# Sample attention: the scores of four sequences issued together, in the four column tiles of the array

## The chip, the cores and the metric

The kernel runs on one core of a Trainium2 chip. The metric is the device time of one launch in microseconds (us). The profiled execution has a time of its own, and its span runs from its first to its last instruction.

## The reference, cut to what matters

One inference step of a two-layer decoder for two request groups with shared weights: a prompt of 512 new tokens, and eight sequences (the sample) with 512 past tokens and four new ones each. Layer A has sparse attention (eight query heads in two key heads, `g` = 0 and 1) beside a gated linear recurrence, layer C is a second recurrence; then a norm. The change is in layer A's attention of the sample. For each sequence `b` and each of two kinds, keys and values come from a paged cache (kind 0, the selected blocks, which are all of them here) or from the sliding window (kind 1):

```python
s = jnp.einsum('qgrd,qgnkd->qgrnk', qg, ks).reshape(qb, HKV, GRP, n_top * L_SEL) * scale
p_s = masked_softmax(s, kpos <= tpos[:, None, None, None])
o_s = jnp.einsum('qgrm,qgmd->qgrd', p_s, vs.reshape(qb, HKV, n_top * L_SEL, DH))
...
s = jnp.einsum('qgrd,kgd->qgrk', qg, wk[:, 0]) * scale
p_w = masked_softmax(s, wmask[:, None, None, :])
o_w = jnp.einsum('qgrk,kgd->qgrd', p_w, wk[:, 1])
o = gx[..., 0:1] * o_c + gx[..., 1:2] * o_s + gx[..., 2:3] * o_w
```

A sequence has 8 heads x 4 tokens = 32 query rows, 16 for each key head; past keys and values have 512 rows of 2 x 128 numbers.

## The kernel before, in words

Everything is float32; the big projections split both operands into two float32r parts and add three products. A weight block is 2048 x 128, its result 128 x 544 (512 prompt tokens and 32 of the sample) in the PSUM tile `gm`. For each of the 16 slices of the contraction six matmuls of 272 columns are issued (`gemm_block`, a *product set* below), and behind each set stands `self.pump()`.

`pump` is a planner. It runs while the program is built and decides the order in which instructions enter the queues. All other work is written as Python generators in lanes; a generator yields the modelled time at which its next step may go (`at`: when the tiles that it reads are modelled as ready, 200 ns later; with `banks` when so many of the four PSUM banks `s` are free). The planner's clock `clk` advances by the modelled cost of each TensorE instruction; after every product set it runs each lane whose time has come. A matmul of at most 32 stationary columns with a `tile_position` is charged 26 + 0.42 n ns (`mm`), a transpose 109. `until` and `force` run the lanes with no products between when the stream can't go on. On the chip nothing of this clock is left: each engine runs its queue in the order written and waits on semaphores for what it reads.

`decode()` is one lane, started when the prompt's attention is done. It treats four items, (group of four sequences, kind) = (0, 0), (1, 0), (0, 1), (1, 1). In an item:

- The keys of a sequence are two page tiles of 128 x 2 x 256 (rows x pages x both key heads), loaded by SP. `fetch()` keeps at most PAGES = 9 tiles in flight or in use, and asks in the order of `feed`: the item's eight key tiles, its eight value tiles, then the next item. A tile counts until `del pages[...]`. A tile of kind 0 is two DMAs (a page each, its address read from the page table), one of kind 1 a single DMA.
- For each sequence `b` and head group `g` four transposes bring the keys to a bank as 128 x 512, a copy (`cp`: ScalarE or VectorE, whichever the planner sees free first) takes them to a tile `kct`, and `scores` multiplies: stationary the queries of the sequence, 128 x 32 (`qd`, zero where a row is of the other head group), moving `kct`, out 32 partitions x 512 of the bank `S`, in column tile `b % 4`. The two head groups add up in the same rows. The score of a step is issued after the copy of the next step (`pend`), so at most two `kct` live.
- Then softmax over `S` (`dm`, `dnm`, `pd`), transposes of `pd`, a copy `ptd`, and the value products, four sequences side by side in the four column tiles, `pg` = 0, 1 with the first half of the value tiles, 2, 3 with the second.

Tiles of type `r` share 17 granules (RGRAN): pages, `kct`, `qd`, `orow` and others, and four split key tiles of the prompt's attention, which `self.khl` holds. When the last item is done, `orow` is transposed, added into `odec`, and the flag `attention` is set; the heads are then gated and split into `oh` and `ol` (`parts`). The stream of blocks meanwhile goes through layer A's last gate projections and on to the output projection `out_blocks`, whose first block takes the recurrence's eight slices first and the eight heads last (`order_a`), and waits for their splits (`ahead_a`).

Of the kernel before, what the change touches and what calls it, by code (L numbers as in the profile page):

```python
# [94 lines left out]
class Kern:  # L95
# [1285 lines left out]
    def decode(self):  # L1381
        nc, ident, a = self.nc, self.ident, self.a
        yield from self.wait("ratt", "gates", "kv10", "kv11", "kvc00", "kvc01", "kvc10", "kvc11")
        yield from self.wait(*[f"pu{h}" for h in range(DECODE_AFTER + 1)])
        yield self.at(self.qd)
        self.odec = self.g("odec", [P, 256])
        orow = self.r("orow", [P, 2, P])
# [2 lines left out]
        for gr, kind in items:  # L1390
            bs = range(4 * gr, 4 * gr + 4)
            feed += [(kind, 0, b, hf) for b in bs for hf in range(2)] + [(kind, 1, b, hf) for hf in range(2) for b in bs]
        pages = {}

        def fetch():
            while feed and len(pages) < PAGES:
                kind, sl, b, hf = key = feed.pop(0)
                if kind == 0:
                    t = self.cache_tile(self.r, 2 + sl, b, hf)
                else:  # L1400
                    t = self.r("pw", [P, 2, 256])
                    src = a["cache_win"][0, b, hf * 256:(hf + 1) * 256, sl].rearrange("(k p) h d -> p k (h d)", p=P)
                    nc.sync.dma_start(t, src)
                pages[key] = t
# [18 lines left out]
        for gr in range(2):  # L1423
            yield self.at(banks=1)
            S = self.bank(reads=2)
            for bl in range(4):
                b = 4 * gr + bl
# [17 lines left out]
            ps = self.bank()  # L1445
# [15 lines left out]
        for gr, kind in items:  # L1461
            bs = list(range(4 * gr, 4 * gr + 4))
            yield self.at(banks=1)
            S = self.bank(reads=2)

            def scores(b, g, t):
                rows = slice(32 * (b % 4), 32 * (b % 4) + 32)
                self.mm(S[rows, :], self.qd[:, g, b, :], t[:, :TP], start=(g == 0), stop=(g == 1),
                        tile_position=(0, 32 * (b % 4)))

            pend = None
            for b in bs:
                ts = [pages[(kind, 0, b, hf)] for hf in range(2)]
                for g in range(2):
                    yield self.at(*ts, banks=1)
                    ps = self.bank()
                    for pg in range(4):
                        self.tr(ps[:, pg * P:(pg + 1) * P], ts[pg // 2][:, pg % 2, g * P:(g + 1) * P], ident)
                    if pend:
                        yield self.at(pend[2], ps)  # L1480
                    else:
                        yield self.at(ps)
                    t = self.r("kct")
                    self.cp(t[:, :TP], ps)
                    if pend:
                        scores(*pend)
                    pend = (b, g, t)
                for hf in range(2):
                    del pages[(kind, 0, b, hf)]
                fetch()  # L1490
            yield self.at(pend[2])
            scores(*pend)
            pend, t = None, None
            yield self.at(S)
            if kind == 1:
                nc.vector.tensor_tensor(S[:, 0:4], S[:, 0:4], self.winneg, op=ALU.add)
            m = self.sm("dm", [P, 2], bufs=2)
            pk = pn[:, gr, kind, :]
            nc.vector.tensor_reduce(m[:, 0:1], S, axis=AX.X, op=ALU.max)
            nc.vector.tensor_reduce(m[:, 1:2], pk, axis=AX.X, op=ALU.max)  # L1500
            nm = self.sm("dnm", [P, 1], bufs=2)
            nc.vector.tensor_reduce(nm, m, axis=AX.X, op=ALU.max, negate=True)
            yield self.at(nm)
            p = self.r("pd")
            s2 = self.sm("ds", [P, 2], bufs=2)
            nc.scalar.activation(p[:, :TP], S, AF.Exp, bias=nm, accum_out=s2[:, 0:1])
            nc.scalar.activation(p[:, TP:T], pk, AF.Exp, bias=nm, accum_out=s2[:, 1:2])
            yield self.at(p, s2)
            sm = self.sm("dsm", [P, 1], bufs=2)
            nc.vector.tensor_tensor(sm, s2[:, 0:1], s2[:, 1:2], op=ALU.add)  # L1510
            w = self.weigh(sm, self.gr[gr][:, 1 + kind:2 + kind])
            wm = self.sm("dwm", [P, 2], bufs=2)
            nc.vector.tensor_scalar(wm, self.gsel, w, None, op0=ALU.mult)
            yield self.at(banks=2)
            ps, ps2 = self.bank(), self.bank()
            for j in range(4):
                self.tr(ps[:, j * P:(j + 1) * P], p[:, j * P:(j + 1) * P], ident)
            self.tr(ps2[:32, :P], p[:, TP:T], ident)
            yield self.at(ps)
            pt = self.r("ptd", [P, 4, P])  # L1520
            self.cp(pt, ps.rearrange("p (j k) -> p j k", k=P))
            ptn = self.sm("ptn", [32, P], bufs=1)
            nc.vector.tensor_copy(ptn, ps2[:32, :P])
            del p, ps, ps2

            new = self.snk if kind == 0 else self.snw[:, 2:4]
            yield self.at(pt, ptn, *[pages[(kind, 1, b, 0)] for b in bs], banks=1)
            O = self.bank(reads=2)
            for pg in range(4):
                if pg == 2:  # L1530
                    for b in bs:
                        del pages[(kind, 1, b, 0)]
                    fetch()
                    yield self.at(*[pages[(kind, 1, b, 1)] for b in bs])
                for b in bs:
                    rc = slice(32 * (b % 4), 32 * (b % 4) + 32)
                    self.mm(O[rc, :256], pt[:, pg, rc], pages[(kind, 1, b, pg // 2)][:, pg % 2, :], start=(pg == 0), stop=False,
                            tile_position=(0, 32 * (b % 4)))
            for b in bs:
                del pages[(kind, 1, b, 1)]  # L1540
                rc = slice(32 * (b % 4), 32 * (b % 4) + 32)
                self.mm(O[rc, :256], ptn[:, rc], new.rearrange("p g d -> p (g d)"), start=False, stop=True,
                        tile_position=(0, 32 * (b % 4)))
            fetch()
            yield self.at(O)
            od = orow[:, gr, :]
            if kind == 0:
                nc.vector.tensor_scalar(od, O[:, 0:P], wm[:, 0:1], None, op0=ALU.mult)
            else:
                nc.vector.scalar_tensor_tensor(od, O[:, 0:P], wm[:, 0:1], od, op0=ALU.mult, op1=ALU.add)  # L1550
            nc.vector.scalar_tensor_tensor(od, O[:, P:2 * P], wm[:, 1:2], od, op0=ALU.mult, op1=ALU.add)
            del pt
        yield self.at(orow, banks=1)
        ps = self.bank()
# [599 lines left out]
```

## Time and profile before

| what | us |
|---|---|
| median of 3 runs | 2389.16 (2386.69 to 2389.62) |
| the profiled execution | 2390.82 |
| its span | 2389.1 |
| TensorE, matmuls busy | 2341.7 |
| TensorE, weight loads busy (beside the matmuls) | 2247.9 |
| VectorE busy | 1382.0 |
| ScalarE busy | 1022.8 |

Matmuls overlap in the array, so the record of one is longer than its turn in the queue: the distance from the start of one instruction to the start of the next tells the turn. In the timeline a row merges instructions of one kind that follow each other: start, time from the first start to the last end, what, and how many records.

### The profile page before, as it was taken

How to read it: one execution, taken by the hardware profiler on the slowest of the kernel's cores; microseconds unless marked ns; L12 is line 12 of the kernel's file. 1: busy time of each engine (PE TensorE's matmuls, PEld its weight loads, DVE VectorE, ACT ScalarE, POOL GpSimd, SP SyncE). 2: the span in 40 equal slices, each digit the busy share in tenths (PEclk: the TensorE clock that was granted, in tenths of full speed). 3: DMA queues.
4: the chain of work that ended last, by engine and by line, in shares of the span. 5: the costliest groups of instructions: out<-in, count | busy, mean ns of one | idle time of the engine just before them, and what ended most of it. 6: DMA issues, size and time to landing. Idle time of an engine off the chain costs nothing.

```text
span 2389.1 us, 49910 instructions
## 1 busy us (share of the span) xinstructions
PE 2341.7 (98%) x20560; PEld 2247.9 (94%) x20560; DVE 1382.0 (58%) x2948; ACT 1022.8 (43%) x2152; POOL 25.7 (1%) x79
## 2 busy tenths in 40 slices
PE   7899999999999999999999999999999999999997
PEld 7799999999999988779999999999999999999997
DVE  5355567774664653354335667777777666665333
ACT  5244344443443443343333445544455444454333
POOL 3000000000000000000000000000000000000000
PEclk9899999999999999999999999999999999999999
DMA  7755434444213135454443233333333333333333
GB/s 247 241 161 158 124 99 109 106 111 119 54 50 89 43 108 163 147 164 134 134 124 98 85 98 101 92 98 90 91 98 94 95 91 91 98 90 113 99 113 111
DMA packets 433612, 270.68 MB, mean 113 GB/s; under 512 B 16285, under 2 KB 419640, under 8 KB 433256
## 3 DMA queue, kind: packets, MB, share of 16 engines
q1 hardware_dynamic: 432520, 257.05, 37.3%
q0 software_dynamic: 256, 8.32, 1.0%
q8 instruction: 162, 2.65, 0.5%
q10 hardware_dynamic: 608, 2.11, 0.2%
q14 instruction: 66, 0.54, 0.1%
HBM read 234.34 MB, written 41.42 MB: 115 GB/s over the span
## 4 chain that ended last, share of the span: by engine, by line
PE 93%; DVE 2%; DMA 1%; SPq 1%; ACT 1%; issue 1%; DVEq 0%; ACTq 0%
PE gm L211 77%; PE s L211 12%; PE s L215 4%; SPq L84 1%; DMA wr<-in_a_w_in_dram 1%; DVE ol L84 1%; DVE wl L84 1%; DMA xres<-res 0%; ACT sq L84 0%; ACT wh L84 0%; DMA wr<-in_a_w_out_dram 0%; ACT e L84 0%; DVE e L84 0%; ACT fr L84 0%; ACT qs L84 0%
## 5 line engine op out<-in xcount | busy, mean ns | idle before, releaser
L211 PE MATMUL gm<-xh,wh 128*128 128x272 f32 x3744 | 814.1, 299 | 1.9 <-ACT wh L84 1.9
L211 PE MATMUL gm<-xh,wl 128*128 128x272 f32 x3744 | 776.1, 289 | 2.7 <-DVE wl L84 2.7
L211 PE MATMUL gm<-xl,wh 128*128 128x272 f32 x3744 | 776.3, 289 | 0.0
L84 DVE TENSOR_TENSOR wl<-wr,wh 128x512 fp32r<-128x512 f32 x660 | 449.8, 686 | 492.4 <-ACT wh L84 491.1
L211 PEld LDWEIGHTS gm<-xh,wh 128*128 128x128 f32 x3744 | 587.1, 189 | 22.7 <-issue 11.6
L84 ACT CAST wh<-wr 128x512 fp32r<-128x512 f32 x660 | 402.4, 616 | 480.7 <-PE gm L211 459.8
L211 PEld LDWEIGHTS gm<-xh,wl 128*128 128x128 f32 x3744 | 588.2, 188 | 3.3 <-DVE wl L84 3.3
L211 PEld LDWEIGHTS gm<-xl,wh 128*128 128x128 f32 x3744 | 589.2, 188 | 0.0
L211 PE MATMUL gm<-oh,wh 128*128 128x272 f32 (+2 forms) x1024 | 219.4, 293 | 3.0 <-ACT oh L84 2.4
L211 PE MATMUL gm<-ol,wh 128*128 128x272 f32 (+2 forms) x1024 | 216.3, 290 | 2.4 <-DVE ol L84 2.4
L211 PE MATMUL gm<-oh,wl 128*128 128x272 f32 (+2 forms) x1024 | 215.7, 289 | 0.0
L211 PEld LDWEIGHTS gm<-oh,wh 128*128 128x128 f32 x1024 | 162.8, 190 | 4.0 <-ACT oh L84 2.9
L211 PEld LDWEIGHTS gm<-ol,wh 128*128 128x128 f32 x1024 | 163.2, 190 | 3.3 <-DVE ol L84 3.3
L211 PEld LDWEIGHTS gm<-oh,wl 128*128 128x128 f32 x1024 | 163.0, 190 | 0.0
L84 ACT ACTIVATE lv<-lv 128x512 f32<-128x512 f32 (+1 forms) x100 | 63.6, 637 | 110.2 <-DVE lv L84 109.5
L211 PE MATMUL gm<-ch,wh 128*128 128x258 f32 (+1 forms) x256 | 76.7, 300 | 1.3 <-ACT ch L84 1.3
L211 PE MATMUL gm<-cl,wh 128*128 128x258 f32 (+1 forms) x256 | 76.8, 300 | 0.8 <-DVE cl L84 0.8
L211 PE MATMUL gm<-ch,wl 128*128 128x258 f32 (+1 forms) x256 | 76.6, 299 | 0.0
L84 DVE TENSOR_TENSOR lv<-b 128x256 f32<-128x256 f32 (+2 forms) x160 | 72.5, 483 | 0.7
L84 ACT ACTIVATE e<-e 128x544 f32<-128x544 f32 x96 | 63.1, 658 | 20.1 <-DVE e L84 18.1
L84 ACT COPY o<-s 128x32 f32<-128x32 f32 (+1 forms) x47 | 18.0, 382 | 108.8 <-PE s L211 108.8
L84 DVE TENSOR_TENSOR rt<-gm,rt 128x544 f32<-128x544 f32 (+2 forms) x33 | 23.4, 708 | 62.2 <-PE gm L211 62.2
(372 smaller groups left out, 2566.8 us busy)
## 6 DMA issues: line engine op xcount, KB each, us to landing
wr<-in_c_w_in_dram SPq DMA_DIRECT2D x128, 512.0 KB
wr<-in_a_w_in_dram SPq DMA_DIRECT2D x104, 512.0 KB
pg<-in_cache_kv_dram SPq DMA_DIRECT2D x128, 128.0 KB
wr<-in_a_cmp_w_dram SPq DMA_DIRECT2D x32, 512.0 KB
wr<-in_a_w_out_dram SPq DMA_DIRECT2D x32, 512.0 KB
wr<-in_c_w_out_dram SPq DMA_DIRECT2D x32, 512.0 KB
out_dram<-s SPq DMA_DIRECT2D x48, 256.0 KB
pw<-in_cache_win_dram SPq DMA_DIRECT2D x32, 256.0 KB
```

What stands on the lines that cost most here:

```text
L84: return f(*args, **kw)
L211: return self.nc.tensor.matmul(out, lhsT, rhs, start=start, stop=stop, **kw)
L215: return self.nc.tensor.transpose(out, in_, ident, **kw)
```

## The change

In an item the loops over `b` and `g` change places. For one head group the keys of all four sequences are transposed and copied to four `kct` tiles, then the four scores are issued one behind the other, each in its column tile; then the same for the other head group. Page tiles of the keys are given back in the second round only, sequence by sequence. A score is no longer issued between the copy and the transposes of two steps; instead the lane waits for all four copies. The four granules of the prompt's split keys are released before the first page is fetched. `scores` itself, the copies, the transposes, the softmax and the value products are the same.

```diff
         yield from self.wait(*[f"pu{h}" for h in range(DECODE_AFTER + 1)])
+        self.khl = None
         yield self.at(self.qd)
...
-            pend = None
-            for b in bs:
-                ts = [pages[(kind, 0, b, hf)] for hf in range(2)]
-                for g in range(2):
+
+            for g in range(2):
+                kct = []
+                for b in bs:
+                    ts = [pages[(kind, 0, b, hf)] for hf in range(2)]
                     yield self.at(*ts, banks=1)
                     ps = self.bank()
                     for pg in range(4):
                         self.tr(ps[:, pg * P:(pg + 1) * P], ts[pg // 2][:, pg % 2, g * P:(g + 1) * P], ident)
-                    if pend:
-                        yield self.at(pend[2], ps)
-                    else:
-                        yield self.at(ps)
+                    yield self.at(ps)
                     t = self.r("kct")
                     self.cp(t[:, :TP], ps)
-                    if pend:
-                        scores(*pend)
-                    pend = (b, g, t)
-                for hf in range(2):
-                    del pages[(kind, 0, b, hf)]
-                fetch()
-            yield self.at(pend[2])
-            scores(*pend)
-            pend, t = None, None
+                    kct.append(t)
+                    if g:
+                        del ts
+                        for hf in range(2):
+                            del pages[(kind, 0, b, hf)]
+                        fetch()
+                yield self.at(*kct)
+                for b, t in zip(bs, kct):
+                    scores(b, g, t)
+                t, kct, ts = None, None, None
             yield self.at(S)
```

## Rows read from the trace of the kernel before

**Rows 1.** The page, busy time of each engine.

```profile
PE 2341.7 (98%) x20560; PEld 2247.9 (94%) x20560; DVE 1382.0 (58%) x2948; ACT 1022.8 (43%) x2152; POOL 25.7 (1%) x79
```

**Rows 2.** The page, chain that ended last, by engine and by line.

```profile
PE 93%; DVE 2%; DMA 1%; SPq 1%; ACT 1%; issue 1%; DVEq 0%; ACTq 0%
PE gm L211 77%; PE s L211 12%; PE s L215 4%; SPq L84 1%; DMA wr<-in_a_w_in_dram 1%; DVE ol L84 1%; DVE wl L84 1%; DMA xres<-res 0%; ACT sq L84 0%; ACT wh L84 0%; DMA wr<-in_a_w_out_dram 0%; ACT e L84 0%; DVE e L84 0%; ACT fr L84 0%; ACT qs L84 0%
```

**Rows 3.** Instructions on tile kct; the last row: idle before them, times.

```profile
L211 PE MATMUL s<-kct,qd x64: 592/593/617, 884.1 to 1041.0; 128*32 128x512 f32 x64
L84 ACT COPY kct<-s x20: 586/587/591, 882.3 to 1035.7; 128x512 f32<-128x512 f32 x20
L84 DVE COPY kct<-s x12: 691/692/692, 883.5 to 1038.0; 128x512 f32<-128x512 f32 x12
...
  ACT kct L84: 0.5, 3
```

**Rows 4.** Timeline of TensorE, 882 to 900 us, first item's scores.

```profile
882.60 0.42 PE L211 MATMUL gm<-xh,wl 128*128 128x272 f32 x2
...
883.21 0.50 PE L211 MATMUL gm<-xh,wh 128*128 128x272 f32 x2
...
883.80 0.41 PE L211 MATMUL gm<-xh,wl 128*128 128x272 f32 x2
884.14 1.05 PE L211 MATMUL s<-kct,qd 128*32 128x512 f32 x2
...
885.53 0.50 PE L211 MATMUL gm<-xh,wh 128*128 128x272 f32 x2
...
897.70 0.41 PE L211 MATMUL gm<-xh,wl 128*128 128x272 f32 x2
898.05 1.90 PE L211 MATMUL s<-kct,qd 128*32 128x512 f32 x4
899.88 0.39 PE L211 MATMUL gm<-xh,wh 128*128 128x272 f32 x1
```

**Rows 5.** Timeline of TensorE, first and last score of the second item.

```profile
933.83 1.04 PE L211 MATMUL s<-kct,qd 128*32 128x512 f32 x2
...
970.16 1.04 PE L211 MATMUL s<-kct,qd 128*32 128x512 f32 x2
```

**Rows 6.** Timeline of TensorE, value products; second row: the window to 911.25 only.

```profile
910.78 0.41 PE L211 MATMUL gm<-xh,wl 128*128 128x272 f32 x2
...
911.12 0.42 PE L211 MATMUL s<-pg,ptd 128*32 128x256 f32 x4
...
911.12 1.07 PE L211 MATMUL s<-pg,ptd 128*32 128x256 f32 x16
912.12 0.52 PE L211 MATMUL gm<-xh,wh 128*128 128x272 f32 x2
912.48 0.41 PE L211 MATMUL gm<-xl,wh 128*128 128x272 f32 x2
...
925.16 1.07 PE L211 MATMUL s<-pg,ptd 128*32 128x256 f32 x16
```

**Rows 7.** Windows: length, PE, PEld, DVE, ACT, POOL busy, clock, DMA share, GB/s.

```profile
884.00:900.00 16.00, 16.00 (x79) 8.45 (x78) 5.90 (x11) 4.67 (x8) 0.00 (x0) 1.00 0.70 201
```

**Rows 8.** Timeline of SP's queue, 886 to 906 us.

```profile
887.14 8.92 SPq L84 DMA_DIRECT2D pg<-in_cache_kv_dram  x8
```

**Rows 9.** Timeline of TensorE, decode's end and output projection; brackets: idle before.

```profile
1053.12 0.38 PE L215 MATMUL s<-ident,orow 128*128 128x128 f32 x2
1053.26 0.50 PE L211 MATMUL gm<-oh,wh 128*128 128x272 f32 x2
...
1060.10 0.52 PE L211 MATMUL gm<-ol,wh 128*128 128x272 f32 x2 [0.32 <-DVE ol L84]
...
1064.48 0.68 PE L211 MATMUL gm<-ol,wh 128*128 128x272 f32 x2 [1.85 <-DVE ol L84]
```

**Rows 10.** Windows, the stretch behind the wait at 1064.48; columns as in rows 7.

```profile
1064.40:1068.00 3.60, 3.52 (x16) 3.51 (x17) 3.60 (x8) 0.00 (x0) 0.00 (x0) 0.54 0.00 0
```

## Prediction

> **What bounds the kernel now.** I read the page first, then the chain of waits, then the rows of the scores alone, and last the end of the layer in which they run. TensorE's matmul side is busy for 2341.7 us, 98% of the span; VectorE has 58%, ScalarE 43% [rows 1]. The chain that ended last is TensorE for 93%: the projections' products (`gm`) 77%, small matmuls through `s` 12%, transposes 4% [rows 2]. So this kernel gets faster by what leaves TensorE's queue, as long as the queue stays full, and the change is a change in that queue.
>
> The scores of sample attention are 32 matmuls of 512 columns; each is recorded as two passes, so they are 64 records of 0.593 us, from 884.1 to 1041.0 us [rows 3]. The record is longer than its turn: in the visit at 898.05, which holds two scores, the four passes end after 1.90 us, the one at 884.14 with two after 1.05, so a pass takes (1.90 - 1.05) / 2 = 0.425 us [rows 4]. The timeline shows how they lie in the queue: six products, one score, four transposes, six products, the next score. There are 30 such visits to 32-column mode, 28 with one score and two with two; the first starts at 884.1, and the last pass of the last at 1041.0 [rows 3].
>
> **The change part by part.** *The scores.* From the product pair at 883.80 to the pair at 885.53 there are one score and one group of four transposes: 1.73 us. From the pair at 882.60 to the pair at 883.21 there is the same group without a score: 0.61. A lone score costs 1.12 us, of which 0.85 are its two passes and 0.27 the way into the mode and out of it [rows 4]. A visit with two, between products, takes 899.88 - 897.70 = 2.18, less the 0.25 that a pair takes anyway, 1.93; the first pair behind such a visit is 0.11 late (912.48 - 912.12 = 0.36 against 0.25), so 2.04 [rows 4, 6]. Before: 28 x 1.12 + 2 x 2.04 = 35.4 us.
>
> The trace of before has no four 512-column scores side by side, but it has the value products of the same attention: eight matmuls of 256 columns, 32 wide, dealt over the four column tiles, 16 passes. Four of them have started before 911.25, and all 16 leave the queue in 912.12 - 911.12 = 1.00 us [rows 6]. One after the other they would need 16 x 0.2125 = 3.4 us, so four run at a time, as four rounds. Four scores of 512 columns are two rounds of double length, the same column count. With its edges that visit costs 912.12 - 910.78 - 0.25 + 0.11 = 1.20 us, and I take this for each group of four. After: 8 x 1.20 = 9.6 us. Saved: 35.4 - 9.6 = 25.8 us. From below the saving is 24 x 0.85 = 20.4, if every switch that goes comes back elsewhere; from above 35.4 - 8 x 0.85 = 28.6, with no edge at all. I take 25.8, since the value products have the edges in them.
>
> *A rule against it.* In order, the second pass of a tile's score would stand in front of the next tile's first, and a group of four would take five pass lengths, 2.1 us + 0.35 of edges, not 1.20. The value products are issued in the same order; in order they would take nine rounds of 0.21, 1.9 us, and took 1.00 [rows 6]. The Trainium skill says (TensorE: Matmul & The Clock Gate, Part 3, section The mechanism) that matmuls start and end strictly in program order; this trace disagrees with that for two-pass matmuls in different tiles, with 1.00 us. By the rule 10 us of the saving would be gone; by the row none. I go by the row.
>
> *Copies and transposes.* 32 groups of transposes and 32 copies stay; a copy takes 0.587 us on ScalarE or 0.692 on VectorE [rows 3]. Taken out from between products, a score leaves transposes between products, which cost no more than their length (above). The copies come closer together: a step is now six products and four transposes, 0.75 + 0.44 = 1.2 us, instead of 2.3. From 884 to 900 us VectorE is busy 5.90 and ScalarE 4.67 of 16 us [rows 7]; the same work in some 12 us is 49% and 39%. The copies keep up. New is that a group of four waits for its last copy with nothing queued in front but what the planner puts there. Before, TensorE waited for a copy 3 times, 0.5 us together, in 30 visits [rows 3]; after it is 8 groups, from 0 to one whole copy each, 0 to 5.5 us. I take 1.0 (twice that row), as the planner waits for the copy's modelled end.
>
> *Pages and granules.* `self.khl = None` gives back four of the 17 granules; nine pages, `qd`, `orow`, four `khl` and two `kct` fill 17 now, and without `khl` there is room for four `kct`. It costs nothing by itself; without it the four key tiles would have no place. Pages are released in the second half of the key phase, not all through it, so the seven value tiles are asked for later. SP issues eight pages in 8.92 us, 1.1 us each, so 14 take some 16 us [rows 8]. In the first item these requests begin at 887.14 now. After, two more steps come behind 884.1 (2.4 us), the last copy and the group (2), and the first step of the second half (1.5): about 890. The last page would then be issued at about 907; the second half of the value products stands at 925.16 [rows 6]. That covers it. In the window items a tile is one issue of 256 KB.
>
> *The order, which is what it costs.* The planner's clock decides behind which product set a step of `decode()` lands. It charges 26 + 0.42 x 512 = 241 ns for a score and goes on charging it, so its total for TensorE is the same, and what I count is added waiting: before each group of four the lane now waits for the last copy, one or two product sets of 0.75 us, twice an item, where before there was one at the item's end. That is 1 to 3 sets an item more, and in the second item, where copies queue behind the gates' work, more. Page waits of the first item take up its share. I put the lane's end at 8 us of product sets later, between 3 and 14. These sets are not lost; they fill the queue. But there is no reserve at the end: the last transposes of `decode()` stand at 1053.12 and the first product of the output projection at 1053.26 [rows 9]. The projection can run 8 sets (6 us) before it needs the heads, and now waits only 0.32 us at 1060.10, then 1.85 at 1064.48 [rows 9]. With the lane 8 us late, the first of these waits grows. It is 6.8 us from the transposes to that product now, with VectorE splitting other rows in between; I allow 4 to 5, as that work is then done. So the wait becomes 8 + 4.5 - 6, about 6, and the one at 1064.48 vanishes: 6 - 0.3 - 1.9, about 4 us lost. Bounds: 0 (lane no later) and 14 + 4.5 - 6 - 2.2, about 10. After the 1.85 us wait the granted clock is 0.54 for 3.6 us, near its level of 1.2 GHz, which loses 1.7 us [rows 10]; that is in the time before already, and a second such dip would add as much.
>
> *Sum.* -25.8 + 1.0 + 4 = -20.8 us, on a span of 2389.1. The profiled execution took 2390.82, 1.7 above the median of the runs; I take the difference off the median: 2389.2 - 20.8 = 2368.4 us.
>
> **The rivals.** *All of it is kept* (the lane ends no later, or the waits at the projection shrink): 2389.2 - 25.8 + 1 - 0 to 2 = 2362 to 2365. For it: the page waits of the first two items can hide new ones. Against it: no reserve at 1053.
>
> *The lane is much later*: 10 to 17 us lost, 2374 to 2382. For it: in the second item the scores already take from 933.83 to 970.16 [rows 5].
>
> *Passes in program order*: 8 x (2.1 + 0.35 - 1.20) = 10 us less saved, 2378. Against it: the 1.00 us of rows 6. *The tiles don't overlap at all*: only the switches of 22 visits go, 22 x 0.27 = 6 us, and 4 to 5 are lost at the end: 2388, no change. The same row speaks against it.
>
> *Slower*: the value pages are asked for half an item later, and their issue at 1.1 us each is exposed in full: 16 us in each of the two page items and some 4 in each of the others, 40 us late at the projection's door. Against it is the 18 us between the last issue and 925.16. It gives 2389.2 - 25.8 + 1 + (40 + 4.5 - 6 - 2.2) = 2401. It decides from a delay of about 29 us on.
>
> **How the numbers follow.** Forecast (2 to 8 us lost at the end, 2366 to 2372): 0.43. All kept, 2360 to 2365: 0.32. Much later, 2372 to 2383: 0.13. Program order: 0.03. No overlap: 0.03. Slower: 0.04; 0.02 is left for what I have not seen. A range of 2359 to 2382 holds the first three almost whole and the fourth; its lower end is the upper bound of the saving (2389.2 - 28.6 = 2360.6) with a little of the waits at the projection, and ending it at 2372 would leave out the term that I can size least. A measurement of this kernel can tell about 0.2%, 4.8 us, from no change. Faster by more (below 2384.4): the first four cases, 0.91. Within: no overlap and what lies between, 0.05. Slower: 0.04.
>
> **What would show it.** The 64 records of `kct`, `qd` stand in eight visits of eight passes, about 1.0 us from the first to the next instruction; together they are busy for about 9 us. Where a visit takes 2 us, program order was right. The place of the `orow` transposes against the first product of `oh` shows how late the lane is, and the waits for `ol` behind it what that costs. I am wrong if that comes true and the span doesn't by as much as I allow: then the queue stood still somewhere between 884 and 1075, for a copy, a page or a split, and the list of waits names it.

## The result and the profile after

The changed kernel takes 2362.05 us (median of 4 runs, 2360.85 to 2364.9), the kernel before 2388.73 in the same company: a ratio of 0.9891, 95% interval 0.9879 to 0.9904, so 26.7 us or 1.1% faster. Forecast were 2368.4, range 2359 to 2382; the number that came is that of the rival *all of it is kept*, though not for the reasons that it gives (below). The profiled execution took 2360.85, its span 2359.1.

The page answers [rows 1]: 31.5 us of busy time are gone from TensorE's matmul side, and its share of the span is what it was.

```profile
PE 2310.2 (98%) x20560; PEld 2239.3 (95%) x20560; DVE 1380.1 (58%) x2946; ACT 1023.2 (43%) x2154; POOL 25.5 (1%) x79
```

The 15072 products of the projections stand in the same order in both traces, so the n-th of one can be laid against the n-th of the other. The 5000th starts 1.21 us earlier than before (a difference that comes from the waits of the first 130 us), the 6000th 27.79 us. In between lies `decode()`, and there 26.6 us were won. In both profiles TensorE waits some 2.4 us between these two products and the granted clock dips once, by 1.7 us; so the 26.6 us are time that the work itself no longer takes in TensorE's queue, not waits and not clock. From there to the last product the lead grows by 2.2 us more, at the start of layer C's output projection: the granted clock fell behind a wait there in the profile of before and not in this one. That fall is not tied to the change: the second profile of the changed kernel (`changed_again`, below) has it too, and there the lead grows by 0.7. With the 1.21 us of the start it makes the two spans differ by 30.0 us where the medians differ by 26.7.

The timeline of TensorE, first item, answers [rows 4]; the last row is the same view cut off at 889.15.

```profile
888.72 0.41 PE L211 MATMUL gm<-xh,wl 128*128 128x272 f32 x2
889.06 1.07 PE L211 MATMUL s<-kct,qd 128*32 128x512 f32 x8
890.06 0.66 PE L215 MATMUL s<-ident,pg 128*128 128x128 f32 x4
890.47 0.50 PE L211 MATMUL gm<-xh,wh 128*128 128x272 f32 x2
...
889.06 0.64 PE L211 MATMUL s<-kct,qd 128*32 128x512 f32 x4
```

Eight records, four scores, leave the queue in 890.06 - 889.06 = 1.00 us. Before, one score took 885.12 - 884.14 = 0.98, from [rows 4] and the row behind it there:

```profile
885.12 0.66 PE L215 MATMUL s<-ident,pg 128*128 128x128 f32 x4
```

Four of the eight passes have started within the first 0.09 us. By the trace's starts they come at 0, 7, 14 and 20 ns, the other four at 454, 460, 467 and 474. I read these as the first passes of the four tiles, then the second passes: the records name no tile, but the two passes of a score alone start 0.45 us apart, and only records of the second four signal that they are done. From pair to pair, less the 0.61 us that the transposes alone take, a visit costs 1.75 - 0.61 = 1.14 us, where a lone score cost 1.12. All eight visits have a turn of 1.00 us.

The instructions on `kct`, answering [rows 3]: the waits for a copy are gone from the list of what these instructions waited for, and the two rows at the end are all that is left there.

```profile
L211 PE MATMUL s<-kct,qd x64: 592/605/617, 889.1 to 1021.1; 128*32 128x512 f32 x64
L84 ACT COPY kct<-s x22: 578/586/589, 881.1 to 1018.1; 128x512 f32<-128x512 f32 x22
L84 DVE COPY kct<-s x10: 691/692/692, 882.3 to 1019.3; 128x512 f32<-128x512 f32 x10
...
  PE s L215: 68.0, 26
  issue: 0.6, 4
```

The end of the lane, timeline of TensorE, answering [rows 9]:

```profile
1022.49 0.41 PE L211 MATMUL gm<-oh,wh 128*128 128x272 f32 x2
...
1031.70 0.73 PE L215 MATMUL s<-ident,orow 128*128 128x128 f32 x2
1034.54 0.51 PE L211 MATMUL gm<-oh,wh 128*128 128x272 f32 x2 [2.11 <-ACT oh L84]
1035.30 0.52 PE L211 MATMUL gm<-ol,wh 128*128 128x272 f32 x2 [0.25 <-DVE ol L84]
```

The last transposes of `decode()` stood 0.14 us ahead of the projection's first product; now they stand 9.2 us behind it. And yet TensorE's idle time here is 2.36 us, against 0.32 + 1.85 and a third wait of 0.24 before.

### The profile page after: what moved, and what is told of

Its sections match the earlier page's. It is cut to its first block, busy times and chain, and to the rows that moved or that the text cites. A ratio compares the mean times of both kernels' runs of the same rounds, so it can differ in the third digit from the quotient of the medians.

```text
span 2359.1 us, 49911 instructions
## 1 busy us (share of the span) xinstructions
PE 2310.2 (98%) x20560; PEld 2239.3 (95%) x20560; DVE 1380.1 (58%) x2946; ACT 1023.2 (43%) x2154; POOL 25.5 (1%) x79
## 3 DMA queue, kind: packets, MB, share of 16 engines
q10 hardware_dynamic: 608, 2.11, 0.2%
## 4 chain that ended last, share of the span: by engine, by line
PE 93%; DVE 2%; ACT 1%; SPq 1%; DMA 1%; issue 1%; DVEq 0%; ACTq 0%
PE gm L211 78%; PE s L211 11%; PE s L215 4%; SPq L84 1%; DMA xres<-res 0%; DVE wl L84 0%; DVE ol L84 0%; DMA ob<-spill 0%; DMA xt<-in_x_sample_dram 0%; ACT e L84 0%; ACT sq L84 0%; ACT wh L84 0%; ACT fr L84 0%; ACT ch L84 0%; ACT qs L84 0%
```

## The experiments

The theory is *overlap*: a visit to 32-column mode costs two pass lengths and its edges, however many of the four column tiles work in it. Its rivals: *switches* (the gain is fewer visits, not tiles at work together) and *order* (it comes from where the lane's steps, page loads and end lie). In the result lines "before" is the kernel before on the same chip, 2386.7 to 2388.0 in these three groups of runs.

**Two scores of one sequence together, in the same column tile.** 16 visits. The edits here are against the changed kernel, where nothing else is said, and leave out unchanged parts ("...").

```diff
-            for g in range(2):
+            for b in bs:
                 kct = []
-                for b in bs:
-                    ts = [pages[(kind, 0, b, hf)] for hf in range(2)]
+                ts = [pages[(kind, 0, b, hf)] for hf in range(2)]
+                for g in range(2):
...
                 yield self.at(*kct)
-                for b, t in zip(bs, kct):
+                for g, t in enumerate(kct):
                     scores(b, g, t)
```

> Scores issued in 16 visits of two, the two head groups of one sequence, which lie in the same column tile; everything else as changed. Overlap theory (the gain is four column tiles working at once): a visit takes 2 x 0.85 + 0.34 = 2.04 us, 16 of them 32.6 us against 35.4 before, so 2.8 us faster than before, about 2386. Switch theory (the gain is that fewer visits enter and leave the 32-column mode): 14 of 30 visits gone against 22 gone in the change, so about 14/22 of the 26.7 us, 17 us faster, 2372. Order theory (the gain comes from where the steps of the lane lie, scores between copy and transposes no more): as the change, 2362.

2380.9 us, ratio to before 0.9973 (0.9964 to 0.9983), 6.4 us faster. A visit's turn is 1.83 us, twice a score:

```profile
881.96 1.90 PE L211 MATMUL s<-kct,qd 128*32 128x512 f32 x4
883.79 0.66 PE L215 MATMUL s<-ident,pg 128*128 128x128 f32 x4
```

Both rivals fail: 14 of the 22 visits are saved, no score stands between copy and transposes, and a quarter of the gain is there. It is more than the 2.8 us that overlap gives, and the rest stands at the projection, where TensorE waits 0.71 + 0.71 us instead of 2.41 and the clock stays at 1.00, which [rows 10] priced at 1.7:

```profile
1051.62 0.38 PE L215 MATMUL s<-ident,orow 128*128 128x128 f32 x2
1053.46 0.52 PE L211 MATMUL gm<-oh,wh 128*128 128x272 f32 x2 [0.71 <-ACT oh L84]
1054.69 0.52 PE L211 MATMUL gm<-ol,wh 128*128 128x272 f32 x2 [0.71 <-DVE ol L84]
```

2.8 + 1.0 + 1.7 = 5.5 of the 6.4.

**Two sequences together, in two column tiles.** 16 visits again.

```diff
-                for b in bs:
+                for n, b in enumerate(bs):
...
-                yield self.at(*kct)
-                for b, t in zip(bs, kct):
-                    scores(b, g, t)
+                    if n % 2:
+                        yield self.at(*kct)
+                        for c, t in zip(bs[n - 1:n + 1], kct):
+                            scores(c, g, t)
+                        kct = []
```

> Scores issued in 16 visits of two, one head group of two sequences, in two column tiles. Overlap theory: each visit is two rounds of 0.425 us and 0.35 of edges, 1.20 us, 19.2 us in all, so 16.2 us faster than before, 2372 to 2373. Passes in program order: three pass lengths and edges, 1.63 us a visit, 26 us, 2379. Switch theory: 17 us faster, 2372, which only the length of a visit tells from overlap. More waits for copies (four an item) may put the lane's end some us later and cost up to 5.

2370.4 us, ratio 0.993 (0.9913 to 0.9947), 16.9 us faster, as overlap has it. The same number of records in a visit as in the run above, in 0.98 us instead of 1.83:

```profile
883.70 1.05 PE L211 MATMUL s<-kct,qd 128*32 128x512 f32 x4
884.68 0.55 PE L215 MATMUL s<-ident,pg 128*128 128x128 f32 x3
```

These two kernels have 16 visits each and differ in whether the two scores share a tile (and in the order of their loops); 10.5 us lie between them. Sixteen visits that are 0.85 us shorter make 13.6; at the projection the kernel with two tiles waits 2.26 us instead of 1.42 and has the clock's dip (0.58 for 4 us, 1.7 us) that the other lacks, which leaves 11.1. Passes in program order would have shown a turn of three pass lengths, 1.3 us and more.

**One by one.** The change's loops and waits, with a product set between two scores.

```diff
                 for b, t in zip(bs, kct):
                     scores(b, g, t)
+                    yield self.later(1.0)
```

> Loops, copies, page releases as in the change, but each score is issued alone, with a product set between two scores. Overlap theory: 32 lone visits of 1.12 us, 35.8 us, all of the gain is gone: 2388, and what the lane's end costs, as 24 more product sets (18 us) pass before it is through: up to 15 more, 2388 to 2403. Order theory: the gain stays, about 2362 to 2366.

2394.2 us, ratio 1.0029 (1.0019 to 1.0039): all of the gain is gone, and 6.8 us more. A score's turn is 0.97 (888.68 to 889.65). *Order* is out. Most of the rest is the late end: the transposes of `orow` come 18.9 us behind the projection's first product, TensorE waits 6.0 us from 1000 us on instead of 2.4 (1.2 of them for a page), and the granted clock costs 3.4 us in two dips instead of 1.7 in one. That is 5.3 of the 6.8.

**All eight scores of an item in one visit**, sequence outside and head group inside as before the change, eight key copies alive, seven pages instead of nine.

```diff
-PAGES = 9
+PAGES = 7
...
+            yield self.at(*kct)
+            for g in range(2):
+                for n, b in enumerate(bs):
+                    scores(b, g, kct[2 * n + g])
```

> All eight scores of an item in one visit (sequence outside, head group inside for transposes and copies; eight key copies live, PAGES 7 instead of 9; the key pages given back sequence by sequence as before the change). Overlap theory: four visits of four rounds, 4 x 0.425 + 0.35 = 2.05 us, 8.2 us against 9.6, 1.4 faster than the change, 2360 to 2361; the lane waits for copies once an item instead of twice. With two pages less in flight TensorE may wait for pages: some us slower than the change, 2363 to 2370.

2365.4 us, ratio 0.9907 (0.9894 to 0.9921): 3 to 5 us slower than the changed program, which took 2359.9 to 2362.1 in its three groups of runs (2359.9 in this group, as the kernel without the release below). The visit is as long as overlap says, four rounds in 894.82 - 892.97 = 1.85 us:

```profile
892.97 1.93 PE L211 MATMUL s<-kct,qd 128*32 128x512 f32 x16
894.82 0.52 PE L211 MATMUL gm<-xh,wh 128*128 128x272 f32 x2
```

But the lane's last item has fallen behind the projection, and TensorE has nothing left to put between its steps; it waits for pages, for the softmax, for the copy of `pd`'s transposes, and for the heads, 6.3 us in all from 1000 us on:

```profile
1012.79 0.41 PE L211 MATMUL gm<-oh,wh 128*128 128x272 f32 x2
...
1019.64 0.44 PE L215 MATMUL s<-ident,pw 128*128 128x128 f32 x2 [0.81 <-DMA pw<-in_cache_win_dram]
1025.24 0.88 PE L215 MATMUL s<-ident,pw 128*128 128x128 f32 x6 [0.61 <-DMA pw<-in_cache_win_dram]
...
1030.43 0.77 PE L215 MATMUL s<-ident,pd 128*128 128x128 f32 x5 [2.17 <-ACT pd L84]
1031.81 3.33 PE L211 MATMUL s<-pw,ptd 128*32 128x256 f32 x32 [0.62 <-ACT ptd L84]
...
1038.35 0.82 PE L211 MATMUL gm<-oh,wh 128*128 128x272 f32 x2 [1.46 <-ACT oh L84]
```

Fewer pages and one wait instead of two were changed at once; which of them made the lane late was not separated.

**The lane made later**, by 2 and by 5 us of planned waiting before each group of four.

```diff
-                yield self.at(*kct)
+                yield self.at(*kct, d=2000.0)    # second kernel: d=5000.0
```

> The change, with 2 us more of planned waiting before each group of four scores, so that two to three more product sets pass each time: about 16 us more in the whole lane, less what the page waits of the first two items take up. TensorE's work is the same. The projection's heads come later than its first eight slices: theory of the prediction (each us later costs a us at the end): 2370 to 2378, shown as a longer wait at the first products of the heads. If the end has a reserve that I don't see: 2362 to 2364.

> As before, with 5 us before each group, about 40 us in the lane, less what page waits take up. Cost us for us: 2362 + 25 to 38, 2387 to 2400, no faster than before the change or slower. With a reserve: below 2380.

2364.3 (ratio 0.99, 0.9885 to 0.9915) and 2369.9 us (0.993, 0.9915 to 0.9945). A planned us costs far less than a us: the planned 16 and 40 us move the lane's end only from 9.2 to 13.8 and 22.1 us behind the projection's first product. That waits for pages take up the rest is likely, but was not measured. The 4.6 and 12.9 us that do arrive cost 2 to 4 us and 8 to 10 against the changed program's 2359.9 to 2362.1. TensorE's waits from 1000 us on are 4.2 and 6.8 us instead of 2.4, and the granted clock dips twice and three times instead of once, which loses 3.4 and some 5 us instead of 1.7. With 5 us, the waits of 6.76 us:

```profile
1016.44 0.49 PE L211 MATMUL gm<-oh,wh 128*128 128x272 f32 x2
1023.94 0.52 PE L211 MATMUL gm<-ol,wh 128*128 128x272 f32 x2 [1.74 <-DVE ol L84]
...
1033.19 0.77 PE L215 MATMUL s<-ident,pd 128*128 128x128 f32 x5 [2.13 <-ACT pd L84]
1034.53 3.15 PE L211 MATMUL s<-pw,ptd 128*32 128x256 f32 x32 [0.57 <-ACT ptd L84]
...
1039.53 0.33 PE L215 MATMUL s<-ident,orow 128*128 128x128 f32 x1 [0.61 <-DVE orow L84]
1041.31 0.51 PE L211 MATMUL gm<-oh,wh 128*128 128x272 f32 x2 [1.46 <-ACT oh L84]
1042.07 0.82 PE L211 MATMUL gm<-ol,wh 128*128 128x272 f32 x2 [0.25 <-DVE ol L84]
```

The three dips of that kernel, windows with the columns of [rows 7]:

```profile
1024.00:1028.00 4.00, 4.00 (x20) 2.28 (x21) 1.90 (x4) 0.48 (x1) 0.00 (x0) 0.61 0.73 219
...
1034.00:1038.00 4.00, 3.48 (x36) 1.49 (x40) 0.44 (x3) 0.47 (x1) 0.00 (x0) 0.64 0.00 0
...
1042.00:1046.00 4.00, 3.93 (x19) 3.93 (x20) 4.00 (x8) 3.62 (x7) 0.00 (x0) 0.58 0.01 4
```

**The granules.** The kernel before with the line `self.khl = None`, and the change without it.

> The kernel before with only the release of the prompt's split key tiles at the start of the lane. All theories that put the gain in the scores: no change, 2388 to 2390. If free granules let pages load earlier and the queue gain from it: some us faster, 2384 or less.

> The change without the release of the prompt's split key tiles. The prediction held that four key copies have no room without it: then copies or page loads wait for granules and the time is some us above 2362. If the granules of tiles that nothing reads any more are taken over anyway: 2362.

2388.6 against 2387.3, ratio 1.0003 (0.9994 to 1.0013); and 2359.9, ratio 0.9885 (0.9869 to 0.99). The change without the line issues the same instructions in the same order on every engine, which is what was expected if the granules of tiles that nothing reads any more are taken over anyway. So it is also one more measurement of the change: between the 5000th and the 6000th product its profile gains 27.9 us.

**The first group's scores behind the next group's first copy**, beside the changed kernel once more.

```diff
-                    yield self.at(ps)
+                    yield self.at(ps, *prev)
...
+                    for c, x in zip(bs, prev):
+                        scores(c, 0, x)
+                    prev, x = [], None
```

> The changed kernel once more, as the neighbour of the next run: 2360 to 2363. The idle of TensorE at the heads' first products about 2.4 us, as before the change; the granted clock falls to about 0.57 behind it in some executions and not in others, which is worth some 1.5 us.

> As the change, but the scores of the first head group are issued after the first copy of the second group, so the lane waits for copies once an item, not twice. The visits stay eight, 1.0 us each. The lane's end should come 3 to 6 us of product sets earlier than in the change, where it lay 9.2 us behind the projection's first product. If the end of the lane still costs something: 1 to 3 us faster than the changed kernel, with less idle before the heads' products. If, as two_same_tile and the late lanes say, the idle is the same 1.4 to 2.4 us for a lane that ends up to some 10 us behind: within 1 us of the changed kernel.

2361.1 (0.9885, 0.9868 to 0.9901) and 2362.6 us (0.9895, 0.9879 to 0.9912): no difference that these runs can tell. The lane's end did not come earlier. The first of the last transposes stands 9.2 us behind the projection's first product in both, and the second waits for VectorE, 2.26 us here and 0.31 in the changed kernel:

```profile
1028.87 0.27 PE L215 MATMUL s<-ident,orow 128*128 128x128 f32 x1
1031.40 0.33 PE L215 MATMUL s<-ident,orow 128*128 128x128 f32 x1 [2.26 <-DVE orow L84]
1033.67 0.51 PE L211 MATMUL gm<-oh,wh 128*128 128x272 f32 x2 [1.94 <-ACT oh L84]
```

So TensorE waits 4.4 us instead of 2.7, and between the 5000th and the 6000th product this profile is 1.8 us longer. The wait for the first group's copies is not what sets the lane's end; what does is not known. No kernel of these is shown to be better than the change.

## Why the prediction was right, point by point

The range held, and the mechanism that the saving rests on. The point forecast was 6.3 us too high: 4 for the lane's end, 1.0 for copies, 0.8 for the scores (26.6 against 25.8) and 0.4 since the kernel before took 2388.7 here and not 2389.2. The number of *all of it is kept*, which had the smaller chance, came by another way than the two that it names: the lane did end later, and the waits at the projection did not shrink by more than 0.1 us.

*The scores.* Right: 35.4 us before, and after eight visits, at 1.14 to 1.20 us each 9.1 to 9.6. The saving of 25.8 to 26.3 is the gain, 26.6 us between the 5000th and the 6000th product (26.4 in the second profile). The value products [rows 6] were the right measure for a shape that the trace of before did not have. One score, two in two tiles and four in four have turns of 0.98, 0.98 and 1.00 us; two in one tile 1.83. That the tiles' overlap causes it is shown by the pair of kernels with 16 visits each.

*Passes in program order.* Right to go by the row: second passes start 0.45 us behind all four first passes. That the trace disagrees with the rule which the prediction sets against it says too much, though. Taken as whole matmuls, the four scores start in the program's order (0 to 20 ns), and so do their second passes (454 to 474 ns). The rule fails only if it is read pass by pass with each score's two passes next to each other, and the records do not show in which order the passes stand in the compiled program.

*Waits for copies.* Allowed 1.0 us, measured 0: no wait of TensorE for `kct` is left. The 0.5 us from which the 1.0 was made had cost nothing either. In the view of [rows 3], under those who waited, they belong to the weight loads, which run beside the matmuls, and no matmul of before waited for `kct`:

```profile
  PEld s L211: 0.5, 3
```

*Pages and granules.* The pages were in time, as worked out: TensorE's matmuls have no wait between 884 and 1000 us. That the four copies have no room without the release was wrong: the program is the same without it.

*The end of the lane.* Here lies the miss. That the lane would end later was right, and 8 us was a good size (9.2 behind the projection's first product). The price of it was wrong: 4 us were allowed, and TensorE's waits went from 2.41 to 2.36 us, that is nothing. Two things were wrong in that term. Behind the projection's first product stand not only 6 us of product sets but the lane's own work, about 3.2 us (transposes of `pd`, value products), which was left out. And the way from the last transposes to the first product with `ol` was allowed 4 to 5 us and took 3.60 (1031.70 to 1035.30; before it was 6.98 by [rows 9], where the prediction has 6.8); to the heads' first product, the one that now waits, it is 2.84. That it is shorter because VectorE has the other slices behind it by then fits, but was not tested. 9.2 + 2.8 - 6.0 - 3.2 = 2.8 us from the last transposes to the heads' first product, which they fill with 0.7 of their own and 2.11 of waiting; with 0.25 behind it that stands in place of the 2.4 of before. So the sum should have been -25.8, 2363.

*The rule that a late lane costs us for us*, from which the rivals *much later* and *slower* had their prices, fails for the first 9 us, which cost nothing. Beyond them it is nearer than the waits alone suggest: of the two late lanes, 4.6 us more cost 2 to 4 and 12.9 more cost 8 to 10, half a us to nearly a whole one for each. About half of that is waiting (1.8 and 4.4 us more than in the change), the rest dips of the clock (1.7 and some 3.4 more). What did not come is the delay: even 40 planned us brought the lane's end only 12.9 us further back. The delay that *slower* has in mind, of the value pages, did not come either: TensorE does not wait for them.

*The clock.* The dip behind the wait at the heads [rows 10] is not a fixed price. The same instructions, with waits of 2.11 and 0.25 us in one execution and 2.11 and 0.24 in another, had it in the first and not in the second (windows of the changed kernel, then of the change without the release):

```profile
1036.00:1040.00 4.00, 4.00 (x22) 4.00 (x21) 4.00 (x7) 3.45 (x7) 0.00 (x0) 0.57 0.01 4
...
```

```profile
1036.00:1040.00 4.00, 4.00 (x34) 4.00 (x34) 4.00 (x7) 2.78 (x6) 0.00 (x0) 1.00 0.01 4
...
```

22 matmuls against 34 in 4 us, at a granted clock of 0.57 and 1.00; between the 5000th and the 6000th product the two executions differ by 1.3 us. The prediction's second dip, "as much" again, did not come with the change, but it is what the later lanes pay.

## What to carry to other kernels

Matmuls like these, which use 32 columns, should enter the queue four at a time, one in each column tile: here a visit with four costs what a visit with one costs (1.14 against 1.12 us), and a matmul of another shape in the same kernel that already does so gives the price beforehand. To see whether a side lane's delay matters, don't count the delay: count everything that TensorE still has to do until it needs the result, the lane's own work included, and compare it with the chain behind the lane's last step. When the queue is full, a wait in a lane costs nothing until the stream has no more work to put in its place; from then on each step of the lane stands bare, as in the kernel with eight scores at once, and the waits can bring dips of the clock that cost about as much again.

## What the runs showed of the hardware

The two passes of a float32 matmul are not held together: with four column tiles in use, four passes start within 20 ns and the other four 0.45 us later, which I read as the first and the second passes of all four tiles, though the program has the scores tile by tile. In a visit of sixteen passes (eight scores) they come in four such rounds, at 0, 0.45, 0.88 and 1.31 us. Two scores in one tile take their four passes one after the other, in 1.83 us. Into the mode and out of it cost 0.27 to 0.35 us a visit, worked out from [rows 4, 6]: the lower between products and transposes, the higher between products on both sides. And the clock's fall behind a wait of 2.1 us can come or stay away for the same program.
